# A two-layer attention-and-retention trunk: fixed rounds for the first supertiles' norms and tables, casts moved to ScalarE, a first rotation read from PSUM

## The chip, the cores and the metric

The kernel runs on one core of a Trainium2 chip. The time is that of one execution on the device, in microseconds (us). Five engines work side by side, each through a list of instructions of its own: TensorE (PE in the profile, its weight loads PEld), VectorE (DVE), ScalarE (ACT), GpSimd (POOL) and SyncE (SP), which issues the DMA transfers. An instruction waits on semaphores for what others must have done, and everything behind it on its engine waits too.

## The reference, cut to what matters

```python
# x (1, 2048, 1024) f32; two layers; rms_norm with a gain; chunks of 64 tokens
def hybrid_layer(x, norm_gain, w_in, w_out, rel_bias, cos, sin):
    hn = rms_norm(x, norm_gain)
    proj = hn @ w_in                                  # 1024 -> 8 sections of 512
    aq, ak, av, ag, rq, rk, rv, rg = jnp.split(proj, cuts, axis=-1)
    ya = chunked_rel_attention(aq, ak, av, rel_bias)  # 8 heads x 64, own chunk and 8 before
    yr = chunkwise_retention(rq, rk, rv, cos, sin)    # 4 heads x 128: rotary on q and k,
                                                      # decay inside a chunk, a running state,
                                                      # rms norm of each head's output
    y = jnp.concatenate([ya * silu(ag), yr * silu(rg)], axis=-1)
    return x + y @ w_out
def reference(x, positions, norm_gain, w_in, w_out, rel_bias, final_gain):
    cos, sin = rotary_tables(positions, RET_HEAD_DIM)
    for layer in range(2):
        x = hybrid_layer(x, norm_gain[layer], w_in[layer], w_out[layer], rel_bias[layer], cos, sin)
    return rms_norm(x, final_gain)
```

## The kernel before

Every large product is made of three float16 products: an operand is scaled by a power of two and split into a high and a low half, and high x high, high x low and low x high are added in PSUM. The scale of a weight section comes from the sum of its squares: ScalarE squares the section and adds up each row (`sumsq`), a cast to bfloat16 follows (`lowp`, on VectorE), one small matmul with ones adds over the 128 partitions (`allsum`), VectorE makes the scale (`norm_scale`), ScalarE writes the scaled high half and VectorE the low half (`convert`).

The 2048 tokens are four *supertiles* `n` of 512, each four tiles of 128 tokens; tile t, of 0 to 15, is called token t in the code's manner below. A layer is four passes `s` over all supertiles; a pass holds two attention heads and one retention head. Stage `(l, s, n)` is `dense_T`, which makes the four sections j = 0 to 3 whose output has features on the partitions (attention queries, attention keys, retention queries, retention keys; 24 matmuls each), and `dense_V`, which makes the values and gates, a section of 24 matmuls for each tile `a` of 128 tokens. Both use two PSUM buffers in turn (`psD`), so a section starts when the one before the last has been emptied: in `dense_V` by four ScalarE activations and three VectorE operations (`rests`, the lines of `v`, `rv` and `gt`). The matmuls of the attention and the retention of the stage before are put in between: `run` takes one step of the dense generator (8 matmuls, a *round*), then fires what `later` has put off to that round, one step of `attention`, and some steps of the background work in `bg`, as many as are needed to end it in time: preparing the next weights (`prep_T`, `prep_V`, `prep_O`), the output weights' maximum (`prep_Omax`), and in the first pass also the norms and the tables of cosines and sines of later supertiles (`norms_from_input`, `tables`).

A rotation (`evacuate`, j = 2 and 3) is made so: ScalarE copies the section out of PSUM into `raw`, two DMAs copy it with its halves exchanged into `swp`, the tables come by two more DMAs (`tab_load`), VectorE makes two products and a sum, and the result is split into halves. For keys a DMA transposes it into tokens (`tokens`).

The first stage is written out by hand, in the string that `do` reads: norms of tiles 0 to 3, the first weights, and the dense sections, as their inputs come. The first supertile's `dense_T` is computed in pieces of 128 tokens for j = 0 and 1. The tokens 4 to 7 follow as background work while the first `dense_V` runs (`push(rounds(...), 12)`), their rows go through a DMA transpose into the layout that `dense_T` reads (`hTh`, `hTl`). Tokens 8 to 15 follow in the stages behind (`push(norms_from_input(...), 21)`), each step with one step of the next table; their rows use the buffers `sc` and `pq` that the attention's scores use too. `decayed` makes the first product of the retention; for the first stage it is called from `attention`, for others from a fixed round.

PE, ACT, DVE and POOL run in the order in which the program is written; SP's order is that of the program in the first stage and a scheduler's afterwards. Names in the profile leave out numbers: `dT` is a section of `dense_T`, `dV` of `dense_V`, `hTh<-hTl` a transpose of rows that lie in a tile of the name `hTl`, `ms` the sum over partitions, `mb` its cast input, `swp` the exchanged halves.

Of the kernel before, what the change touches and what calls it, by code (L numbers as in the profile page):

```python
# [27 lines left out]
def hybrid_trunk(ctx: ExitStack, tc: tile.TileContext, x, pos, gain, gcol, w_in, w_out, rel, fgain,  # L28
# [107 lines left out]
    TAB_STEPS = 19  # L136

# [23 lines left out]
    def gain_scale(l):  # L161
# [7 lines left out]
        mb = lowp(ss, f"g{l}")  # L169
# [8 lines left out]
        mb = lowp(ss, f"h{l}")  # L178
# [126 lines left out]
    def sumsq(sts, nm, dst):  # L305

        m1 = b2.tile([P, len(sts)], F32, tag="m1", name=f"m1{nm}", bufs=4)
        for i, (st, k0, k1) in enumerate(sts):
            act.activation(st if dst is None else dst[:, k0:k1, :], st, AF.Square, accum_out=m1[:, i:i + 1])
        if len(sts) == 2:  # L310
            dve.tensor_tensor(m1[:, 0:1], m1[:, 0:1], m1[:, 1:2], op=ALU.add)
        return m1[:, 0:1]

    def lowp(m1, nm):
        mb = b2.tile([P, 1], BF16, tag="mb", name=f"mb{nm}", bufs=4)
        dve.tensor_copy(mb, m1)
        return mb

# [32 lines left out]
    class Sections:  # L351
# [16 lines left out]
        def square(self, j):  # L368
            nm = f"{self.nm}{j}"
            self.sq[j] = lowp(sumsq(self.sts[j], nm, self.g.h[:, j]), nm)  # L370
# [43 lines left out]
    def prep_V(l, s, g):  # L414
# [25 lines left out]
        for j in range(2):  # L440
            yield
            m1[j] = lowp(sq(j), f"{nm}{j}")
# [9 lines left out]
        m3 = sq(3)  # L452
        dve.tensor_tensor(m2, m2, m3, op=ALU.add)
        m2 = lowp(m2, f"{nm}2")
# [10 lines left out]
    def prep_V_next(l, g):  # L465
# [13 lines left out]
        m = [lowp(sumsq(sts[j], f"{nm}{j}", hi[j]), f"{nm}{j}") for j in range(2)]  # L479
        yield  # L480
        m2, m3 = (sumsq(sts[j], f"{nm}{j}", hi[j]) for j in (2, 3))
        dve.tensor_tensor(m2, m2, m3, op=ALU.add)
        m.append(lowp(m2, f"{nm}2"))
# [10 lines left out]
    def prep_Omax(l, go):  # L494
        nm = f"O{l}"
        mm = b2.tile([P, 1], F32, tag="omax", name=f"omax{nm}")
        st = load_sec(w_out[l, :, 0:P], f"{nm}m0")
        for j in range(KT):
            yield
            m1 = sumsq(st, f"{nm}m{j}", None)  # L500
            if j + 1 < KT:
                st = load_sec(w_out[l, :, (j + 1) * P:(j + 2) * P], f"{nm}m{j + 1}")
            if j == 0:
                dve.tensor_copy(mm, m1)
            else:
                dve.tensor_tensor(mm, mm, m1, op=ALU.add)
        mm = lowp(mm, nm)
        for _ in range(4):
            yield
# [98 lines left out]
    def dense_T(l, s, n, g, st):  # L608
# [17 lines left out]

        def evacuate(j, ps):
# [27 lines left out]
            else:  # L655
                w = 5 - j
                rot = b2.tile([P, w, 512], F16, tag=f"rot{j}", name=f"rot{nm}_{j}")
                if j == 2:
# [5 lines left out]
                def swap(rot=rot, raw=raw, j=j):  # L664
# [20 lines left out]
                    d = 5 if j == 2 and first else 3  # L685
# [7 lines left out]
                    else:  # L693
                        later(d + 5 if first else 11, tokens)

                if j == 2:
                    st.rq = rot
                    swap()
                    if first:
                        later(1, tab_load)  # L700
                else:
                    st.rk = rot
                    later(8 if first else 2, swap)
# [14 lines left out]
        for j in range(2 if first else 0, 4):  # L718
            if j == 2 and not first:
                tab_load()  # L720
# [57 lines left out]
    def attention(l, s, n, g, st, prev, nxt):  # L778
# [61 lines left out]
        for i, (a, hx) in enumerate(units):  # L840
# [11 lines left out]
            elif a == 0 and (l, s, n) == (0, 0, 0):  # L852
                decayed(l, s, n, g, st, 0)
# [297 lines left out]

    def run(gen, att, thirds):
        left = thirds
        for _ in gen:
# [3 lines left out]
            ring["att_done"] = att[0] is None  # L1158
            todo = sum(max(b[1], 0) for b in bg)
# [6 lines left out]
    def norms_from_input(ts, spaces, tab):  # L1166

        def load(k):
            u = us[k]
            u.x = spaces[k] if spaces else w4.tile([P, D], F32, tag="w4", name=f"xin{u.t}")  # L1170
            sp.dma_start(u.x, x[u.t * P:(u.t + 1) * P, :])

        def sq(k):
            u = us[k]
            u.h = [h_[:, :, u.t % 4 * P:(u.t % 4 + 1) * P] for h_ in hT_of(0, u.t // 4)]
            u.ss = squares(u.x.rearrange("p (k c) -> p k c", c=P), u.nm, u.h[0])

        def root(k):
            us[k].rs = rms_of(us[k].ss, gains[0].m, gains[0].e, us[k].nm)

        def mul(k):
            u = us[k]
# [333 lines left out]
```

## Time and profile before

| | us |
|---|---|
| median of 3 runs | 2095.43 (2093.11 to 2095.86) |
| the profiled execution | 2094.75 |
| its span, first to last instruction | 2092.8 |
| mean granted TensorE clock | 0.991 |
| TensorE busy in the span | 2004.4 |
| VectorE, ScalarE, GpSimd busy | 1343.8, 1141.3, 432.9 |

The profile is of one execution. Busy time is given for each engine; a row of a timeline has the start, the time that the merged instructions took, engine, source line, operation, what is written from what, the shapes, the count, and in brackets how long the engine stood idle before and what ended that. A group has busy time, the mean of one in ns, and the idle time before its instructions. The lines that carry the argument stand in the prediction.

### The profile page before, as it was taken

To read this page: it belongs to the slowest core of one execution; us is meant where nothing else is said; L and a number is where in the kernel's file an instruction comes from. 1 tells how busy PE (TensorE), PEld (TensorE's weight loads), DVE (VectorE), ACT (ScalarE), POOL (GpSimd) and SP (SyncE) were. 2 spreads that over 40 slices of the span, in tenths; PEclk is the share of its full clock that TensorE was granted. 3 is DMA by queue.
4 is the path that set the end of the run, shared out by engine and by line. 5 is a ranking of instruction groups with operands and counts; after the bars stand their busy time and mean duration, and the time that the engine had idled before them with its cause. 6 is when DMAs were issued, how large, how long until landed. Compare 5 with 4: busy or idle time off the path is not lost.

```text
span 2092.8 us, 39599 instructions
## 1 busy us (share of the span) xinstructions
PE 2004.4 (96%) x14014; PEld 1049.4 (50%) x14014; DVE 1343.8 (64%) x4031; ACT 1141.3 (55%) x2522; POOL 432.9 (21%) x509
## 2 busy tenths in 40 slices
PE   6888999999999999998999999999999999998998
PEld 4344455555555555444444555555555555554443
DVE  7676666666656666576654666666666667656643
ACT  7455665556565654455444546554655565455432
POOL 1022222222122212121000222222222222222100
PEclk9999999999999999999999999999999999999999
DMA  8767674557476764599965556655655776558874
GB/s 247 171 127 162 136 166 114 115 112 159 110 169 133 161 166 99 113 211 260 219 185 113 120 102 142 130 121 106 155 123 118 178 156 162 117 100 183 212 199 123
DMA packets 645702, 313.65 MB, mean 150 GB/s; under 512 B 459232, under 2 KB 602080, under 8 KB 645504
## 3 DMA queue, kind: packets, MB, share of 16 engines
q1 hardware_dynamic: 645504, 311.12, 66.4%
q8 instruction: 110, 1.80, 0.4%
q14 instruction: 88, 0.72, 0.1%
HBM read 123.26 MB, written 41.98 MB: 79 GB/s over the span
## 4 chain that ended last, share of the span: by engine, by line
PE 55%; DMA 7%; DVE 5%; ACT 3%; issue 1%; SPq 1%; POOL 0%; POOLq 0%; DVEq 0%; ACTq 0%
PE dT L731 18%; PE dV L752 15%; PE dO L1105 12%; DMA pT<-pq 2%; PE r L860 2%; PE S L801 2%; PE S L800 2%; PE o L820 1%; PE o L821 1%; PE o L822 1%; DVE sc L804 1%; DMA swp<-rot 1%; DMA yhy<-rhy 1%; ACT sc L807 1%; ACT pq L809 1%
## 5 line engine op out<-in xcount | busy, mean ns | idle before, releaser
L810 POOL TENSOR_TENSOR pq<-sc,pq 128x640 f16<-128x640 f32 (+4 forms) x256 | 323.8, 1265 | 1175.9 <-issue 590.7
L807 ACT ACTIVATE sc<-sc,mq,cT 128x640 f32<-128x640 f32 (+4 forms) x256 | 218.5, 853 | 558.1 <-DVE mq L806 413.7
L752 PE MATMUL dV<-whV,hTh 128*128 128x512 f16 x1024 | 354.5, 382 | 13.0 <-DVE gt L770 12.8
L731 PE MATMUL dT<-hTh,whT 128*128 128x512 f16 x1008 | 349.4, 382 | 14.7 <-DMA hTh<-hTl 9.6
L752 PE MATMUL dV<-wlV,hTh 128*128 128x512 f16 x1024 | 354.1, 381 | 0.0
L752 PE MATMUL dV<-whV,hTl 128*128 128x512 f16 x1024 | 354.0, 381 | 0.0
L731 PE MATMUL dT<-hTl,whT 128*128 128x512 f16 x1008 | 346.6, 379 | 0.0
L731 PE MATMUL dT<-hTh,wlT 128*128 128x512 f16 x1008 | 346.6, 379 | 0.0
L752 PEld LDWEIGHTS <-hTh 128*128 128x128 f16 x2048 | 197.3, 98 | 227.7 <-DVE gt L770 16.4
L731 PEld LDWEIGHTS <-whT 128*128 128x128 f16 x2016 | 192.9, 98 | 221.6 <-issue 24.1
L804 DVE CUSTOM_DVE_ANT_0 sc<-S,bias 128x640 f32<-128x640 f32 (+4 forms) x256 | 188.4, 736 | 78.8 <-PE S L801 61.1
L1105 PE MATMUL dO<-whO,yly 128*128 128x512 f16 x512 | 194.1, 379 | 2.4 <-DMA yly<-rly 2.4
L1105 PE MATMUL dO<-whO,yhy 128*128 128x512 f16 x512 | 194.0, 379 | 1.2 <-DVE gt L770 0.6
L1105 PE MATMUL dO<-wlO,yhy 128*128 128x512 f16 x512 | 194.0, 379 | 0.0
L809 ACT ACTIVATE pq<-sc 128x640 f16<-128x640 f32 (+4 forms) x256 | 171.5, 670 | 10.9 <-DMA pT<-pq 3.0
L1105 PEld LDWEIGHTS <-yhy 128*128 128x128 f16 x1024 | 99.6, 98 | 115.1 <-issue 0.8
L752 PEld LDWEIGHTS <-hTl 128*128 128x128 f16 x1024 | 99.7, 98 | 105.0 <-issue 2.8
L800 PE MATMUL S<-k,q 128*128 128x128 f16 (+3 forms) x592 | 143.1, 268 | 7.9 <-DVE mq L804 7.9
L731 PEld LDWEIGHTS <-wlT 128*128 128x128 f16 x1008 | 97.2, 98 | 101.8 <-issue 1.1
L820 PE MATMUL o<-v,pT 128*128 128x65 f16 x1120 | 129.6, 193 | 10.2 <-DMA pT<-pq 9.7
L801 PE MATMUL S<-k,q 128*128 128x128 f16 (+3 forms) x592 | 130.5, 268 | 0.0
L820 PEld LDWEIGHTS <-pT 128*128 128x128 f16 x1120 | 105.3, 97 | 49.2 <-DMA pT<-pq 21.3
(350 smaller groups left out, 3352.7 us busy)
## 6 DMA issues: line engine op xcount, KB each, us to landing
q<-qq SPq DMA_DIRECT2D x128, 128.0 KB, 2.7
yyy<-y_d SPq DMA_DIRECT2D x32, 512.0 KB, 4.6
stT<-in_w_in_dram SPq DMA_DIRECT2D x27, 512.0 KB, 4.8
stV<-in_w_in_dram SPq DMA_DIRECT2D x26, 512.0 KB, 4.5
k<-kk SPq DMA_DIRECT2D x128, 64.0 KB, 2.0
swp<-rot SPq DMA_DIRECT2D x64, 128.0 KB, 2.5
tabc<-tab SPq DMA_DIRECT2D x32, 256.0 KB, 2.7
tabs<-tab SPq DMA_DIRECT2D x32, 256.0 KB, 2.9
```

The lines of the kernel that those rows point to most:

```text
L731: pe.matmul(ps, w_[:, j, kt, :], h_[:, kt, :], start=(m == 0), stop=(m == 23))
L752: pe.matmul(ps, h_[:, kt, a * P:(a + 1) * P], w_[:, kt, :], start=(m == 0), stop=(m == 23))
L800: pe.matmul(o, st.q[:, hx, 0, cs], k_, start=True, stop=False)
L801: pe.matmul(o, st.q[:, hx, 1, cs], k_, start=False, stop=True)
L804: dve.tensor_tensor_reduce(out=v, in0=S[:, 0:w], in1=g.bias[hx][:, 640 - w:640], scale=1.0, scalar=-3.0e38, op0=ALU.add, op1=ALU.max, accu ...
L807: act.activation(v, v, AF.Exp, bias=m[:, 0:1], scale=g.c[:, 0:1])
L809: act.activation(pq[:, 0:w], v, AF.Copy)
L810: pool.tensor_tensor(pq[:, w:2 * w], v, pq[:, 0:w], op=ALU.subtract)
L820: pe.matmul(o[:, 0:65], u.p[:, b, :], v_[:, 0:65], start=(b == 0), stop=False)
L821: pe.matmul(o[:, 0:64], u.p[:, b, :], v_[:, 65:129], start=False, stop=False)
L860: pe.matmul(out_, w_, m_, start=(i == 0), stop=(i + 1 == len(pairs)))
L1105: pe.matmul(ps, h_[:, kt, :], w_[:, kt, :], start=(m == 0), stop=(m == 23))
```

## The change

Casts: `lowp` becomes a ScalarE activation; where a sum has two parts the second is added as its bias, and the VectorE addition is dropped (in `gain_scale` the cast stays on VectorE). `prep_Omax` keeps the eight sums of squares in eight columns, loads two sections ahead, adds them with one reduction, and is spread over the whole of the stage `n` = 2.

```diff
     def lowp(m1, nm, more=None):
         mb = b2.tile([P, 1], BF16, tag="mb", name=f"mb{nm}", bufs=4)
-        dve.tensor_copy(mb, m1)
+        if more is None:
+            act.activation(mb, m1, AF.Copy)
+        else:
+            act.activation(mb, m1, AF.Identity, bias=more[:, 0:1])
         return mb
...
     def prep_Omax(l, go):
+        ms = b2.tile([P, KT], F32, tag="omax", name=f"omax{nm}", bufs=1)
+        load(0)
+        load(1)
+        yield
         for j in range(KT):
-            yield
-            m1 = sumsq(st, f"{nm}m{j}", None)
-            if j + 1 < KT:
-                st = load_sec(w_out[l, :, (j + 1) * P:(j + 2) * P], f"{nm}m{j + 1}")
-            if j == 0:
-                dve.tensor_copy(mm, m1)
-            else:
-                dve.tensor_tensor(mm, mm, m1, op=ALU.add)
+            if j + 2 < KT:
+                load(j + 2)
+            yield
+            act.activation(st[j], st[j], AF.Square, accum_out=ms[:, j:j + 1])
+            yield
+        yield
+        dve.tensor_reduce(m1, ms, axis=AX.X, op=ALU.add)
```

First rotation: for the first stage the two products read the section in PSUM; the exchange of halves is made by the output's partitions, in two operations of 64 partitions each, and the copy out of PSUM and the four DMAs fall away. `decayed` of the first stage moves to round 10, that is into `dense_V`.

```diff
+        def first_rotation(j, ps, rot):
+            def cosine():
+                dve.scalar_tensor_tensor(out=own, in0=ps, scalar=2.0 ** -16, in1=st.tabc, op0=ALU.mult, op1=ALU.mult)
+            def sine(half):
+                i_, o_ = slice((1 - half) * 64, (2 - half) * 64), slice(half * 64, half * 64 + 64)
+                dve.scalar_tensor_tensor(out=st.swp[o_], in0=ps[i_], scalar=-2.0 ** -16, in1=st.tabs[i_], op0=ALU.mult,
+                                         op1=ALU.mult)
+            d = 2 * j
+            later(d, cosine)
+            later(d, lambda: sine(0))
+            later(d + 1, lambda: sine(1))
+            later(d + 2, lambda: dve.tensor_tensor(own, own, st.swp, op=ALU.add))
+            later(d + 3, lambda: act.activation(rot[:, 0], own, AF.Copy))
+            later(d + 4, lambda: dve.tensor_tensor(rot[:, 1], own, rot[:, 0], op=ALU.subtract))
```

Second supertile: j = 0 and 1 of stage (0, 0, 1) are made in pieces of 128 tokens, those of tokens 4 to 6 ahead of those of token 7, and both are emptied behind the last piece.

```diff
+        parts = (l, s, n) == (0, 0, 1)
+        if parts:
+            for (j, a) in ((0, 0), (0, 1), (0, 2), (1, 0), (1, 1), (1, 2), (0, 3), (1, 3)):
+                cs = slice(a * P, (a + 1) * P)
+                for i in range(24):
+                    w_, h_ = ((g.h, hh), (g.l, hh), (g.h, hl))[i // KT]
+                    pe.matmul(ps[j][:, cs], w_[:, j, i % KT, :], h_[:, i % KT, cs], start=(i == 0), stop=(i == 23))
+                    m += 1
+                    if m % 32 == 0 and m < 192:
+                        yield
+                if a == 3:
+                    evacuate(j, ps[j])
```

Fixed rounds: `run` counts rounds from the first `dense_V` on and fires what `slot` has put on a round. Up to round 95 the background work is pulled from there alone. A token's steps stand on set rounds (load 4 rounds ahead of its square, rows three to five rounds behind it), tokens 8 to 11 from round 18 and 12 to 15 from round 39, every three rounds; their rows lie in space of their own. The steps of the tables 1, 2 and 3 have set rounds, and the weights of pass 1 are prepared from round 57 on, 48 steps over 39 rounds.

```diff
+            for fn in slots.pop(ring["round"], ()):
+                fn()
+            ring["round"] += 1
+            if left is None:
+                continue
...
+            for i, fn in ((-4, load), (0, sq), (1, root), (2, mul), (3, lambda: rows_hi(rows, u.x)),
+                          (4, lambda: rows_lo(rows, u.x)), (5, lambda: transpose_rows(rows, *u.h))):
+                slot(r + i, fn)
+        for k, t in enumerate(ts):
+            v = rows[k % len(rows)].bitcast(F16)
+            token(t, r0 + 3 * k, (v[:, 0:D], v[:, D:2 * D]))
...
+    table_steps(t1, (12, 12, 13, 13, 14, 15, 17, 17))
+    table_steps(t2, [18] + list(range(22, 36)) + [36, 38, 38])
+    table_steps(t3, [36] + list(range(40, 54)) + [54, 56, 56])
+    norms_from_input(18, range(8, 12), late[0:4])
+    norms_from_input(39, range(12, 16), xs0[0:2])
+    first_prep = 57
+    for r in range(first_prep, 96):
+        for _ in range((r + 1 - first_prep) * 48 // 39 - (r - first_prep) * 48 // 39):
+            slot(r, lambda: pull(1))
+    slot(first_prep - 1, lambda: push(prep_T(0, 1, grp(0, 1)), 25))
...
-                if (l, s) == (0, 0) and 0 < n < NS - 1:
-                    if n == 1:
-                        push(t1, TAB_STEPS - 10)
-                    push(norms_from_input(range(4 * n + 4, 4 * n + 8), late[0:4] if n == 1 else None,
-                                          tables(n + 1, [xs0[n + 1][:, i * 256:(i + 1) * 256] for i in range(4)])), 21)
...
-                if (n, s) == (0, 0) and not first:
+                if (n, s) == (0, 0):
                     later(11, lambda n=n, g=g, st=st: decayed(l, s, n, g, st, 0))
```

154 lines of the change are left out of this document (82 added, 72 removed).

## The prediction

> **What bounds the kernel now.** I read the page's first part, then the busy time of each engine by stage, then who TensorE waited for in the early stages, then the timelines of the engines named there.
>
> ```profile
> PE 2004.4 (96%) x14014; PEld 1049.4 (50%) x14014; DVE 1343.8 (64%) x4031; ACT 1141.3 (55%) x2522; POOL 432.9 (21%) x509
> ```
>
> TensorE is the bound: of the span of 2092.8 us it is idle 88 us. The columns below are the stretch, its length, and the busy time (and count) of PE, PEld, DVE, ACT and POOL, the granted clock, the DMA share and GB/s. The cuts are mine: the wait after the first supertile, the second supertile, the third, the fourth with what follows, the rest.
>
> ```profile
> 69.10:78.90 9.80, 0.17 (x1) 0.02 (x1) 2.47 (x7) 1.21 (x4) 0.00 (x0) 0.62 1.08 241
> 78.90:140.10 61.20, 51.66 (x292) 24.67 (x292) 46.40 (x135) 35.14 (x75) 10.86 (x18) 0.95 0.62 130
> 140.10:204.90 64.80, 55.23 (x399) 29.32 (x399) 46.54 (x127) 36.24 (x76) 15.61 (x18) 0.94 0.74 154
> 204.90:360.00 155.10, 147.09 (x1081) 77.87 (x1082) 100.76 (x361) 94.09 (x217) 34.56 (x41) 0.99 0.65 141
> 360.00:2092.80 1732.80, 1698.38 (x11852) 885.03 (x11849) 1094.34 (x3264) 926.89 (x2061) 364.84 (x411) 1.00 0.66 147
> ```
>
> Between 69.1 and 360 us TensorE idles 9.6 + 9.5 + 9.6 + 8.0 = 36.7 us. In the 1732.8 us behind that it idles 34.4 us, and the change touches little there. The waits of TensorE from 60 to 142 us, from 142 to 206 and from 206 to 360 (total, times, longest):
>
> ```profile
> PE dT L731 <- DMA hTh<-hTl: 9.6, 1, 9.6
> PE dV L752 <- DVE gt L770: 5.5, 2, 4.9
> PE dT L731 <- issue: 2.2, 1, 2.2
> ...
> PE dV L752 <- DVE gt L770: 4.8, 2, 4.3
> PE dT L731 <- DMA hTh<-rhn: 2.8, 1, 2.8
> ...
> PE msT L323 <- DVE mbT L316: 3.3, 3, 1.9
> PE msV L323 <- DVE ya L832: 2.9, 2, 1.6
> ```
>
> Norm rows that land late, value sections whose accumulator VectorE empties late, and a sum that waits for a cast on VectorE: the places that the change edits. A wait also costs afterwards (start, duration, [idle before]):
>
> ```profile
> 78.91 3.26 PE L731 MATMUL dT<-hTh,whT 128*128 128x512 f16 x8 [9.64 <-DMA hTh<-hTl]
> ...
> 82.11 1.89 PE L731 MATMUL dT<-hTh,wlT 128*128 128x512 f16 x8
> ...
> 140.13 1.89 PE L731 MATMUL dT<-hTh,whT 128*128 128x512 f16 x8 [2.21 <-issue]
> ...
> 204.90 3.40 PE L731 MATMUL dT<-hTh,whT 128*128 128x512 f16 x8 [2.81 <-DMA hTh<-rhn]
> ```
>
> Eight matmuls take 1.89 us, but 3.26 and 3.40 behind waits of 9.64 and 2.81 us, and 1.89 behind one of 2.21: between 2.21 and 2.81 us the clock is halved for a while. By the clocks of the table that is 3.1 us of the second supertile (5% of 61.2; 1.4 of them at 78.91) and up to 3.9 of the third (6% of 64.8), of which I take 2.6, since a part of the slow stretch falls into the wait itself; and 1.5 at 204.9 (3.40 against 1.89). So 36.7 + 7.2 = 43.9 us are lost between 69 and 360 us.
>
> **The first rotation and the parts.** The change takes four copies by DMA and the loads of tokens 8 to 11 out of SP's queue ahead of the last rows of tokens 4 to 7.
>
> ```profile
> 70.71 0.57 SPq L1171 DMA_DIRECT2D hTh<-in_x_dram  x1
> ...
> 71.86 0.50 SPq L666 DMA_DIRECT2D swp<-raw  x1
> ...
> 73.10 1.53 SPq L236 DMA_TRANSPOSE hTh<-hTl  x1
> 74.73 2.92 SPq L237 DMA_TRANSPOSE hTl<-hTl  x1
> ```
>
> Those last two transposes end the 9.64 us wait; DMA engines are full (1.08) just there. Their rows were ready long before:
>
> ```profile
> 58.10 1.22 DVE L276 TENSOR_TENSOR hTh<-hTh,hTh 128x1024 f16<-128x1024 f32 x1
> 59.24 0.69 DVE L670 TENSOR_TENSOR rot<-rot,tabc 128x512 f32<-128x512 f32 x1
> ...
> 60.98 1.28 DVE L254 SCALAR_TENSOR_TENSOR hTl<-hTl,rsn,gb 128x1024 f32<-128x1024 f32 x1
> 62.17 0.68 DVE L670 TENSOR_TENSOR swp<-swp,tabs 128x512 f32<-128x512 f32 x1
> 62.77 0.28 DVE L766 SCALAR_TENSOR_TENSOR v<-dV,v 128x128 f16<-128x128 f32 x1
> ...
> 64.16 1.22 DVE L276 TENSOR_TENSOR hTl<-hTl,hTl 128x1024 f16<-128x1024 f32 x1
> ```
>
> By the new order of VectorE the queue turns around here. From start to start an L276 takes 1.14 us, an L254 1.19, a 512-wide product 0.60. Ahead of the second value section's evacuation (L766 at 62.77) stood two L276, one L254 and two products; now two L276, one L254 and six products or sums (first rotation: cosine, two halves of the sine, sum; second: cosine, one half). That is 58.10 + 2.28 + 1.19 + 3.65 = 65.2, and 0.8 for the evacuation: 66.0. The fourth section needs that accumulator:
>
> ```profile
> 63.93 0.38 PE L752 MATMUL dV<-whV,hTh 128*128 128x512 f16 x1
> ...
> 68.89 0.38 PE L752 MATMUL dV<-wlV,hTh 128*128 128x512 f16 x1
> ```
>
> So it starts at 66.0 instead of 63.9: a new wait of 2.1 us. The first decay product moves ahead too, behind two thirds of that section (69.5), and needs the second rotation. VectorE after 66.0: a sine half 0.6, L276 1.14, a lower part 0.6, a sum 0.6, two table steps 0.6, an evacuation 0.8, three table steps 0.95, the lower part 0.6: 71.9. A second wait, 2.4 us. The section ends at 66.0 + 5.2 + 2.4 = 73.6. The last rows are ready at 67.8, so two transposes of 1.3 us and some 3 us of flight put them at 71 to 73: no wait is left for the parts to save. TensorE goes on at 73.6 instead of 78.9: **-5.3**, and -1.4 of clock (3.26 against 1.89). Bounds: -11 if VectorE keeps up, 0 if it loses another 5 us.
>
> The products now read PSUM. The same 512-wide form from PSUM is in the groups:
>
> ```profile
> L634 DVE SCALAR_TENSOR_TENSOR qq<-dT,qq 128x512 f16<-128x512 f32 x32 | 21.9, 683 | 12.4 <-ACT qq L631 12.4
> ```
>
> 683 ns, like the 0.69 and 0.68 from SBUF above, so I charge nothing more. [...]
>
> The parts: 192 matmuls of 128 columns for 48 of 512.
>
> ```profile
> 30.73 0.61 PE L712 MATMUL dT<-hTl,whT 128*128 128x128 f16 x8
> 31.18 0.61 PE L712 MATMUL dT<-hTh,wlT 128*128 128x128 f16 x8
> ```
>
> Eight take 0.45 us start to start: 192 take 10.8 against 48 x 0.216 = 10.4. **+0.4**.
>
> **Norms and tables in rounds, rows apart.** The work is the same; its rows no longer take the two buffers of the attention's scores, and the Sin step of the third supertile's table leaves the value sections:
>
> ```profile
> L121 ACT ACT_TABLE_LOAD x3 | 3.8, 1283 | 0.0
> ```
>
> One such load and one back, 2.6 us, stood ahead of the evacuation behind the 4.9 us wait. What is left is VectorE's load. Second supertile: TensorE's own work is 51.7 - 3.1 = 48.6 us; VectorE's is 46.4 less the second rotation's 2.6, so 90% of it. I also see a new jam: sixteen SP issues of the table, the queries and the keys (0.5 to 0.6 us each, as the rows above) stand ahead of the table's reload, some 5 us that VectorE waits at the first cosine. That uses the slack up, so I keep half of what was lost there (9.5 + 1.7 of clock): 5.5. **-5.7**. Third: 55.2 - 2.6 = 52.6 against 46.5, without that jam, and its successor's rows are ready seven rounds ahead; lost 9.6 + 2.6 + 1.5, kept 5: **-8.7**. Fourth and next: lost 8.0, weight work spread over 39 rounds; kept 4: **-4.0**. Bounds: all of it gone, or all of it kept.
>
> **Casts by ScalarE.** Five casts in the start and 51 behind it leave VectorE.
>
> ```profile
> L316 DVE CAST mbT<-m1T 128x1 bf16<-128x1 f32 x28 | 4.4, 156 | 36.9 <-ACT whT L309 36.7
> ```
>
> VectorE stood 36.7 us idle behind the squares for these casts alone. On ScalarE the cast follows its square at once; the sum on TensorE comes three rounds later. Hidden by those rounds behind 360 us, where VectorE is 63% busy: 0. Bounds -2 to +3.
>
> **The output weights' maximum.** Its running sum held VectorE behind a square that waited for a load, and TensorE behind that:
>
> ```profile
> 623.55 0.19 DVE L506 TENSOR_TENSOR omaxO<-omaxO,m1O0m 128x1 f32<-128x1 f32 x1 [3.14 <-ACT stO0m L309]
> ```
> ```profile
> PE r L860 <- DVE dT L868: 2.4, 2, 1.3
> ...
> PE msO L323 <- DVE yr L925: 1.3, 2, 0.7
> ```
>
> These two waits, once a layer, are 3.7 us; with columns, one reduction and loads two ahead I keep 1.1: **-2.6**. Bounds -3.7 to +1.
>
> **The sum** against the profiled execution's 2094.75 us (1.95 around its span): -5.3 - 1.4 + 0.4 - 5.7 - 8.7 - 4.0 - 2.6 = -27.3, so 2067.5. The median shown is 0.7 above that execution: 2068.
>
> **Rivals.** (1) VectorE binds the second and third supertile, at 90% of TensorE's own work: what was lost there (11.2 + 13.7) stays, only the other terms gain, 12.9: 2083 with the 0.7. For it: every new wait I found ends on VectorE. Against: its idle time behind ScalarE goes. 0.22. (2) No wait is left between 63 and 360 us: 43.9 + 3.7 - 0.4 gained: 2048. For it: the DMA and buffer couplings named in the waits are cut. Against: the two waits worked out above. 0.09. (3) It does not do what it says: VectorE is so late that the rows and the decay product come when they did, and later waits move one supertile on: 2095. 0.07. (4) Slower: the sums wait for casts in ScalarE's queue, behind exponentials and Sin. Each of the three mbT waits cost 1.1 us (3.3 over 3); 51 casts at that price are 56 us, less the 27.3: 2124. It decides from 0.54 us a cast. Against: ScalarE is 53% busy behind 360 us and the sum comes three rounds after. 0.10. [...]
>
> **How the numbers follow.** The forecast has 0.52 and a range of its own from 2058 to 2078. 2054 to 2090 takes in rival 1, and leaves out most of 2, 3 and 4. A measurement tells 0.2%, 4 us, from no change. Faster: 0.52 + 0.22 + 0.09 = 0.83; same: 0.07; slower: 0.10.
>
> **What would show it.** Right: the fourth value section of the first supertile starts near 66 us, a wait of 2 to 3 us stands before the first decay product, the first part starts at 72 to 75 us without a wait for rows; the third supertile starts near 128 and the fourth near 183; no wait for the maximum above 1 us. Wrong: waits for `gt` of 4 us and more with half clock behind them, a wait of the parts for transposes, or sums that wait for ScalarE's cast in the later stages.

## The result and the profile after

The changed kernel is slower, by a third of a per cent, where the forecast was 27 us faster.

| | before | after |
|---|---|---|
| median, us | 2095.43 (19 runs, 2090.72 to 2100.03) | 2102.21 (19 runs, 2096.17 to 2105.39) |
| ratio after to before, 95% interval | | 1.0034 (1.0026 to 1.0043) |
| profiled execution, us | 2094.75 | 2103.35 |
| its span, us | 2092.8 | 2101.6 |
| mean granted clock | 0.991 | 0.993 |

The ratio is taken between runs of the two kernels on the same chip. The page's first part of after, and its row of the DMA queue of kind "instruction" (packets, MB, share), which comes up again below:

```profile
PE 2009.7 (96%) x14158; PEld 1058.0 (50%) x14158; DVE 1339.1 (64%) x3950; ACT 1151.0 (55%) x2576; POOL 433.2 (21%) x509
...
q8 instruction: 111, 1.82, 0.4%
```

The parts show as 144 more matmuls. VectorE has 81 instructions fewer and ScalarE 54 more, most of it the casts (e1 below, which has the casts alone, has 69 fewer and 56 more). Now the busy time by stage of after, cut where the prediction cut it, at the places where the supertiles begin here (columns as there):

```profile
60.00:75.70 15.70, 10.76 (x51) 4.54 (x50) 15.27 (x30) 5.96 (x14) 0.58 (x4) 1.00 0.80 165
75.70:135.76 60.06, 50.72 (x434) 30.36 (x433) 42.19 (x124) 31.09 (x71) 10.22 (x15) 0.97 0.56 124
135.76:200.11 64.35, 55.00 (x399) 28.53 (x399) 44.34 (x125) 38.26 (x78) 16.11 (x17) 0.97 0.82 175
...
357.00:2101.60 1744.60, 1701.84 (x11874) 886.09 (x11872) 1090.75 (x3209) 937.74 (x2109) 363.28 (x411) 1.00 0.66 147
```

TensorE still idles 60.06 - 50.72 = 9.3 us in the second supertile (9.5 before) and 9.4 in the third (9.6). Behind 357 us it idles 42.8, where before it idled 34.4 behind 360. The waits of TensorE in after, from 60 to 142 us, 142 to 206, 206 to 330, and in the stretch of the first layer's maximum, 575 to 640 (total, times, longest):

```profile
PE dV L819 <- DVE gt L837: 4.7, 2, 2.7
PE S L867 <- DVE mq L871: 3.4, 3, 2.7
PE dT L798 <- DVE ya L899: 3.0, 1, 3.0
PE r L925 <- DVE rot L668: 2.0, 1, 2.0
...
PE S L867 <- DVE mq L871: 2.7, 2, 2.1
PE dV L819 <- DVE gt L837: 2.3, 2, 2.1
PE dT L798 <- DVE gt L837: 2.2, 1, 2.2
...
PE msV L327 <- DVE yr L990: 2.6, 1, 2.6
PE dV L819 <- ACT whV L334: 2.2, 1, 2.2
...
PE o L887 <- DMA pT<-pq: 1.6, 2, 1.1
```

The 9.64 us for late rows is gone, and so is every wait of 4 us and more. In their place stand many of 2 to 3 us, and up to 206 us all that are shown end on VectorE. VectorE is at work while TensorE stands there: of the 17.8 us of TensorE's waits over half a microsecond that end between 75.7 and 200.2 us it is busy for 16.2. Before, of the 28.4 us that end between 78.9 and 205 us, it was busy for 11.3. In TensorE's timeline of after:

```profile
67.76 0.39 PE L819 MATMUL dV<-whV,hTh 128*128 128x512 f16 x1 [2.70 <-DVE gt L837]
...
73.91 0.23 PE L925 MATMUL r<-rot,rot 128*128 128x128 f16 x1 [2.03 <-DVE rot L668]
...
75.70 0.61 PE L775 MATMUL dT<-hTh,whT 128*128 128x128 f16 x8
...
135.76 1.89 PE L798 MATMUL dT<-hTh,whT 128*128 128x512 f16 x8 [2.97 <-DVE ya L899]
...
283.42 0.16 PE L327 MATMUL msV<-mbV,ones 128*128 128x1 bf16 x1 [2.63 <-DVE yr L990]
...
291.64 3.47 PE L819 MATMUL dV<-whV,hTh 128*128 128x512 f16 x8 [2.23 <-ACT whV L334]
```

The second supertile starts at 75.70 instead of 78.91, the third at 135.76 instead of 140.13, the fourth at 200.11 instead of 204.90. The dense products of stage (0,1,0), which follows the fourth supertile, end at 318.7 before and 319.0 after: the whole lead is given back in that one stage. From there to the end is 1774.1 before and 1782.6 after. By the prediction's terms, as differences of these places:

| stretch | predicted | measured |
|---|---|---|
| up to the second supertile's start (78.91, 75.70) | -5.3 | -3.2 |
| second supertile (61.20, 60.06 long) | -1.4 + 0.4 - 5.7 = -6.7 | -1.1 |
| third (64.80, 64.35) | -8.7 | -0.5 |
| fourth and (0,1,0), to 318.7 and 319.0 | -4.0 | +5.1 |
| from there to the end (1774.1, 1782.6) | -2.6 | +8.5 |
| sum | -27.3 | +8.8 |

The last row is the largest miss: a stretch that the change was said to touch little. Most of its +8.5 lies in the five stages that open a pass with loaded bias tables, (0,2,0), (0,3,0), (1,1,0), (1,2,0) and (1,3,0), each from the end of one stage's value sections to the end of its own: 265.7 us together before, 271.7 after.

### The profile page after: what moved, and what is told of

Same layout as the page of the kernel before. It is cut to its first block, busy times and chain, and to the rows that moved or that the text cites. A ratio compares the mean times of both kernels' runs of the same rounds, so it can differ in the third digit from the quotient of the medians.

```text
span 2101.6 us, 39837 instructions
## 1 busy us (share of the span) xinstructions
PE 2009.7 (96%) x14158; PEld 1058.0 (50%) x14158; DVE 1339.1 (64%) x3950; ACT 1151.0 (55%) x2576; POOL 433.2 (21%) x509
## 3 DMA queue, kind: packets, MB, share of 16 engines
q8 instruction: 111, 1.82, 0.4%
## 5 line engine op out<-in xcount | busy, mean ns | idle before, releaser
L798 PE MATMUL dT<-hTh,whT 128*128 128x512 f16 x992 | 342.9, 380 | 6.0 <-DVE ya L899 3.0
L867 PE MATMUL S<-k,q 128*128 128x128 f16 (+3 forms) x592 | 142.4, 267 | 11.8 <-DVE mq L871 11.8
L933 DVE SCALAR_TENSOR_TENSOR sh<-sh,state 128x128 f16<-128x128 f16 x120 | 96.1, 801 | 66.6 <-ACT sh L929 66.4
```

The source lines that it names most:

```text
L798: pe.matmul(ps, w_[:, j, kt, :], h_[:, kt, :], start=(m == 0), stop=(m == 23))
L867: pe.matmul(o, st.q[:, hx, 0, cs], k_, start=True, stop=False)
L933: dve.scalar_tensor_tensor(out=dst[:, 1], in0=dst[:, 0], scalar=-2.0 ** 11, in1=src, op0=ALU.mult, op1=ALU.add)
```

## Experiments

The ratios are taken against the kernel before on the same chip. The medians come from several chips, on which before alone took 2094.86 to 2097.6, so that they can't be compared with each other; "five stages" is that sum of lengths in the run's trace. Each run's profile is one execution, whose time behind 319 us scatters by some us, so that a verdict rests on the ratio and its interval, and the trace says where.

**Casts.** e1 is the kernel before with the first hunk of the change alone; e2 is after with that hunk undone.

```diff
-        dve.tensor_copy(mb, m1)
+        if more is None:
+            act.activation(mb, m1, AF.Copy)
+        else:
+            act.activation(mb, m1, AF.Identity, bias=more[:, 0:1])
```

> The kernel before with one edit alone: the casts by ScalarE (and the second part of a sum as the cast's bias). My prediction charged this edit 0 (bounds -2 to +3). Theory A (SP's queue): this edit alone moves one store in SP's order, y_d11<-ya, from behind the transpose pT of unit (3, 0, 1) and the first key copies to ahead of them, at the start of each later pass; the store waits for VectorE, and TensorE waits behind it, as at 699.32 and 1508.05 us in the changed kernel (2.86 and 2.48 us). Then this kernel takes 5 to 9 us more than the kernel before, 2100 to 2104, and its trace has waits of o for DMA pT at the starts of passes. Theory B (casts are free, the loss comes from other parts): 2095 within 2. Theory C (sums wait for the cast itself in ScalarE's queue): also slower, but the waits are of msT and msV for ACT mb.

> The changed kernel with the casts put back on VectorE; everything else of the change stays. Theory A: SP's order at the pass starts is the old one again, the 8 us lost behind 355 us come back: 2093 to 2096. Theory B: 2102. If VectorE's load in the second and third supertile matters, the casts there cost less than 1 us.

e1: 2097.9, 1.0006 (0.9997 to 1.0015). e2: 2103.14, 1.0034 (1.0022 to 1.0045), as after. The casts cost nothing that can be told from 0, by either way; the slow-down is elsewhere.

**SP's order.** In after SP issues a store of attention output ahead of a transpose of scores that TensorE waits for; e3 holds that store back.

```diff
+                i = sp.dma_start_transpose(out=u.p, in_=pq[:, 0:2 * w])
+                if (n, a, hx) == (3, 0, 1):
+                    tc.keep_in_program_order(i)
...
+                    if n == 2 and u.a == 3:
+                        later(4, store)
```

> The changed kernel with its casts on ScalarE, but the store of ya (supertile 2, tile 3) issued four rounds later and held behind the transpose of unit (3, 0, 1) in SP's order; nothing else moves. Theory A: the waits for pT at 521, 596, 699, 733, 1508 us go: 2093 to 2097. Theory C: the casts themselves cost the time, so it stays at 2101 to 2103.

2106.49, 1.0045 (1.0032 to 1.0058), five stages 273.1: no gain. SP's order there isn't the cause.

**Weights of pass 1 earlier.** 

```diff
-    first_prep = 57
+    first_prep = 51
```

> The changed kernel with the weights of pass 1 prepared from round 51 instead of 57, at the same rate, so done by round 90 instead of 95. Theory D: the lead of 7.3 us that the change has at 255 us is lost in stage (0, 1, 0) because the last conversions end only as their dense_V starts: the waits at 283.42 and 291.64 us (2.63 and 2.23) and the halved clock behind both (some 1.7 each) go, and the time falls by 5 to 8 us, to 2094 to 2097. Rival E: the weights' work meets the third supertile's norms six rounds sooner on VectorE and loses there what it gains: 2101 to 2103.

2110.21, 1.0063 (1.0051 to 1.0076). The waits of 2.63 and 2.23 us go and stage (0,1,0) takes 55.5 us for 60.7. But the third and fourth supertile grow by 10.5 together: from 190 to 330 us e4's waits of TensorE begin with

```profile
PE msT L327 <- ACT mbT L315: 11.5, 2, 8.7
```

a sum that stands 8.7 us for ScalarE's cast. That is rival 4's mechanism, in a place where the change as it stands does not have it (1.2 at most). So the weight work can be put against one stage or the other, and what it needs is not free in either.

**Semaphores.** SP's transfers use eight completion semaphores in turn (in the traces 1402 transfers before and 1398 in after, 174 to 176 on each); the change could have turned which transfer shares one with which. Four tiny loads, whose data nothing uses, are added in (0,1,1), to after (e5) and to before (e6).

```diff
+                if (l, s, n) == (0, 1, 1):
+                    for k in range(4):
+                        later(8 + k, lambda k=k: tiny(k))
```

> The changed kernel with four tiny loads (128 x 1) added in stage (0, 1, 1), behind the keys' copies; nothing else moves. Transfers take eight completion semaphores in turn, and the change issues four transfers fewer in the first stage (the two exchanges of halves of the first rotations), so that every later transfer has another of the eight than before. Theory F: that turn sets how long the same chain of transfers takes at the start of a pass (kt, toep, toep, bias, weights, pT), and thereby the waits of o for pT at 521, 596, 699, 733 and 1508 us. With four loads more the turn is the old one again: the loss of about 8 us behind 355 us goes, 2094 to 2097. Rival G: the turn has nothing to do with it: 2102 to 2104, at most 2 us slower for the four issues.

> The kernel before with the same four tiny loads at the same place. Theory F: it takes on the changed kernel's turn of semaphores and loses 5 to 8 us at the starts of the passes: 2100 to 2104. Rival G: 2095 to 2098.

e5: 2107.48, 1.005 (1.0036 to 1.0065), five stages 272.2. e6: 2100.62, 1.0019 (1.0009 to 1.0028), five stages 265.6. e6 is 0.2% slower than before, clear of noise and inside the 2100 to 2104 that the theory gave for it; where it loses these 4 us isn't known. But its five stages are as long as before, and the same loads do not shorten after's: for the five stages, which it was to explain, the theory falls.

**VectorE's waits in the second supertile.** e7 issues the table loads at once, where `tab_load` was put off by three rounds; e8 moves the subtraction that makes the low rows of tokens 8 to 15 to GpSimd.

```diff
-                if (l, s) == (0, 0):
-                    later(3, tab_load)
-                else:
-                    tab_load()
+                tab_load()
```
```diff
-                          (4, lambda: rows_lo(rows, u.x)), (5, lambda: transpose_rows(rows, *u.h))):
+                          (4, lambda: pool.tensor_tensor(rows[1], u.x, rows[0], op=ALU.subtract)), (5, lambda: transpose_rows(rows, *u.h))):
```

> The changed kernel with the reload of the tables in the first pass at once, not three rounds later. VectorE's wait of 5.50 us for tabc at 103.19 us goes. Theory H (VectorE's one wait makes it late for what TensorE needs): the waits of S for mq at 110.23 (2.72) and of the fourth value section at 125.42 (2.00) shrink, with the half clock behind the first (1.7): 3 to 5 us ahead at 140 us, and as much at the third supertile. Rival I: VectorE is late for the sum of its work, and the waits only move: within 1 us at 140 us. In the whole time 0 to 8 us less than 2102.

> The changed kernel with the lower halves of the norms' rows of tokens 8 to 15 subtracted by GpSimd instead of VectorE: eight operations of 1.2 to 1.6 us leave VectorE in the second and third supertile (6 us in each). Rival 1 of the prediction (VectorE's load binds there): the idle time of TensorE in these two stages (6.2 and 10.3 us in the changed kernel) falls by 2 to 5 us each, 2094 to 2098. Rival I' (it is the order and the latency of single steps, VectorE being idle a quarter of that time): less than 1 us each, 2100 to 2103.

e7: 2109.84, 1.0063 (1.0047 to 1.0078), slower even than after. e8: 2105.08, 1.0038 (1.0024 to 1.0053). VectorE's longest wait between 78 and 140 us, in after and then in e7:

```profile
DVE rot L720 <- DMA tabc<-tab: 5.5, 1, 5.5
```
```profile
DVE rot L720 <- DMA swp<-rot: 6.5, 1, 6.5
```

The wait for the table, which the prediction had foreseen as some 5 us, goes, and the one for the exchanged halves behind it comes in its place, longer. In e8, TensorE's waits from 60 to 142 us:

```profile
PE dV L819 <- DVE gt L837: 5.9, 3, 2.7
PE dT L798 <- DMA hTh<-hTl: 3.4, 1, 3.4
PE S L867 <- DVE mq L871: 2.5, 3, 1.8
```

With less work on VectorE the waits for it stay, and one for rows joins them. So it isn't VectorE's load alone; no single edit tried here shortened the stage.

**Place of buffers.** The change moves later buffers down by 32 bytes (`bufs=1` of `omax`). e9 takes that back in after, e10 makes it in before.

```diff
-        ms = b2.tile([P, KT], F32, tag="omax", name=f"omax{nm}", bufs=1)
+        ms = b2.tile([P, KT], F32, tag="omax", name=f"omax{nm}")
```
```diff
-        mm = b2.tile([P, 1], F32, tag="omax", name=f"omax{nm}")
+        mm = b2.tile([P, 1], F32, tag="omax", name=f"omax{nm}", bufs=1)
```

> The changed kernel with one word less: the eight sums of the output weights' maximum in two buffers, as the one sum had before (bufs=1 is dropped). All instructions and their order on every engine stay as in the changed kernel. What moves is where buffers lie: in the changed kernel everything allocated behind that small tile (weights, rows' transposes hT, bias, the loads' space w4) begins 32 bytes lower in each partition than in the kernel before, at 32 over a multiple of 64, and with this word at a multiple of 64 as before. Theory J (place of the buffers): transfers into these buffers take longer at an odd multiple of 32, and the chains of transfers at the starts of the passes with them; the waits of o for pT at 521 to 733, 1291 and 1508 us go, and the time falls by 5 to 10 us, to 2093 to 2097. Rival K (the place does not matter): 2101 to 2104.

> The kernel before with one word more: that small tile in one buffer (bufs=1). All instructions and their order stay; the buffers behind it lie 32 bytes lower, as in the changed kernel. Theory J: it loses 6 to 12 us, most of it at the starts of the passes, with waits of o for pT of 1 to 3 us: 2101 to 2108. Rival K: 2095 to 2097.

e9: 2106.19, 1.0044 (1.0031 to 1.0056). e10: 2096.61, 0.9999 (0.999 to 1.0008). Nothing.

**Instruction fetches.** The pages' rows of the queue of kind "instruction", before and in e12 (below), beside after's above:

```profile
q8 instruction: 110, 1.80, 0.4%
```
```profile
q8 instruction: 112, 1.84, 0.4%
```

These are 110, 111 and 112 packets of 16 KB. TensorE's matmuls and weight loads are 2 x 14014 = 28028 and 2 x 14158 = 28316, and in e12 2 x 14270 = 28540: 255 to a packet in all three. With the 163 and 168 instructions of TensorE's sequencer they are 28191 before and 28484 in after, 256.3 and 256.6 to a packet. The starts of the packets are 17.7 and 17.8 us apart in the median. From these counts, not from the packets' size as the expectation of e11 has it, I read a packet as a fetch of TensorE's next instructions, and estimate 256 to a fetch. The parts put in 288 = 256 + 32 instructions, so that by this estimate each later fetch comes 32 instructions sooner. Counted from the issue of the first bias load (`toep`) in each of the five stages, fetches stood at 13.1 to 13.6 us in the first layer and 4.6 to 5.2 in the second; in after they stand at 9.5 to 10.6 and 0.0 to 0.2, upon transfers that a chain waits for. The DMA view of after, in a short stretch around that issue in stage (1,2,0) (queue and what it moved; then issues with KB and us from issue to landing):

```profile
q8 instruction: 1, 0.02, 3.7%
...
toep<-rel_d SPq DMA_DIRECT2D x1, 383.5 KB, 6.4
kt<-rot SPq DMA_TRANSPOSE x1, 4.7
```

and the same place before, where no row of that queue stands:

```profile
q1 hardware_dynamic: 1352, 0.39, 85.7%
...
toep<-rel_d SPq DMA_DIRECT2D x2, 383.5 KB, 5.0
kt<-rot SPq DMA_TRANSPOSE x1, 3.2
```

A fetch takes 1.03 us in the median, and here `kt` lands 1.5 us later. The other traces agree: at the starts of (1,1,0), (1,2,0) and (1,3,0) `kt` lands 3.1 to 3.4 us from its issue in all ten traces of this document with the fetches in the old place, and 4.2 to 4.9 us in all nine with them moved. SP's queue behind it, before (start, duration):

```profile
1487.93 1.39 SPq L683 DMA_TRANSPOSE kt<-rot  x1
...
1494.26 0.34 SPq L577 DMA_DIRECT2D bias<-toep  x1
...
1495.53 2.74 SPq L812 DMA_TRANSPOSE pT<-pq  x1
```

and after:

```profile
1492.54 1.40 SPq L733 DMA_TRANSPOSE kt<-rot  x1
...
1500.40 0.33 SPq L588 DMA_DIRECT2D bias<-toep  x1
...
1501.33 3.28 SPq L879 DMA_TRANSPOSE pT<-pq  x1
```

`bias` was issued as the first `toep` landed (1494.25 before, 1500.39 in after), with the transpose of scores behind it on SP: from `kt` to `pT` are 7.60 us before and 8.79 after, and `o` waits for `pT`. To tell the fetches from the parts' own work, tiny matmuls of one column on ones, whose results nothing uses, are put at the very start: 144 of them in before (e11, the parts' number), 112 in after (e12: 224 instructions, which with 288 make 512, two whole packets by the estimate). e13 is after without the parts, hence with the count of before.

```diff
+    for i in range(4):
+        wp = psR.tile([P, 512], F32, tag="small", name=f"wp{i}")
+        for _ in range(36):
+            pe.matmul(wp[:, 0:1], ones.to_broadcast([P, P]), ones, start=True, stop=True)
```
```diff
+    for i in range(4):
+        wp = psR.tile([P, 512], F32, tag="small", name=f"wp{i}")
+        for _ in range(28):
+            pe.matmul(wp[:, 0:1], ones.to_broadcast([P, P]), ones, start=True, stop=True)
```
```diff
-        parts = (l, s, n) == (0, 0, 1)
+        parts = False
```

> The kernel before with 144 matmuls of one column (ones x ones) ahead of everything, in the first microseconds, where TensorE stands idle for 5.18 us; nothing else moves. They are as many instructions as the parts of the second supertile add (192 matmuls for 48, each with its weight load: 288). Theory L (instruction fetch): a DMA queue of kind instruction moves 16 KB about every 18 us, 1.03 us each, 110 of them; by their size these are TensorE's instructions, 256 at a time, and 288 more move each such fetch some 32 instructions ahead: from 13 to 10 us and from 5 to 0 us behind the toep copies at the starts of the passes, into the flight of kt and pT. Then this kernel gets the changed kernel's late transfers, with waits of o for pT: it loses 4 to 8 us behind 355 us, 2100 to 2105. Rival M (what makes the transfers late is another part of the change): 2095 to 2099, at most 2 us slower for the tiny matmuls.

> The changed kernel with 112 such tiny matmuls at the start: with the 288 instructions of the parts these make 512 more than before, twice 256, so that the fetches fall where they fell before. Theory L: the waits of o for pT at 521, 596, 699, 733, 1291, 1508 us go, the loss behind 355 us with them: 2094 to 2098. Rival M: 2101 to 2105.

> The changed kernel without the parts: j = 0 and 1 of the second supertile as whole sections again; all else stays, and TensorE has as many instructions as before. Theory L: the fetches fall where they fell before, 2093 to 2098 in all. For the parts themselves: the last rows land at 71 to 73 us and TensorE came at 75.70, so the second supertile still starts without a wait above 1 us, and is 0.4 us shorter. Rival M: 2101 to 2104. If the parts did hide rows, a wait for hTh or hTl of 2 us and more stands at the start of the second supertile.

| | fetches | median, us | ratio | five stages, us |
|---|---|---|---|---|
| before | old place | 2095.43 | | 265.7 |
| e11 | moved | 2099.01 | 1.0009 (0.9998 to 1.0021) | 271.1 |
| after | moved | 2102.21 | 1.0034 (1.0026 to 1.0043) | 271.7 |
| e12 | moved back | 2095.95 | 0.9993 (0.9984 to 1.0003) | 268.3 |
| e13 | moved back | 2098.43 | 1.0007 (0.9996 to 1.0017) | 267.9 |

The same place in e11 has the fetch and the long flight, in e12 neither:

```profile
q8 instruction: 1, 0.02, 2.8%
...
toep<-rel_d SPq DMA_DIRECT2D x2, 383.5 KB, 5.7
kt<-rot SPq DMA_TRANSPOSE x1, 4.3
```
```profile
toep<-rel_d SPq DMA_DIRECT2D x2, 383.5 KB, 5.3
kt<-rot SPq DMA_TRANSPOSE x1, 3.2
```

Over 360 to 1900 us TensorE's waits for `pT` are, before, after and in e12:

```profile
PE o L820 <- DMA pT<-pq: 8.4, 9, 2.2
```
```profile
PE o L887 <- DMA pT<-pq: 16.7, 13, 2.9
```
```profile
PE o L891 <- DMA pT<-pq: 13.8, 11, 2.5
```

e12 does more work than after and is faster, its interval wholly below after's; e13 gets there by leaving the parts out, and in e11 the same kind of useless matmuls works the other way, on the flights and the five stages of the kernel before. What the three have in common is the count alone, so the place of the fetches is a cause. The other runs bear it out. The eight versions of the changed kernel with moved fetches have ratios of 1.0034 to 1.0063, the six with the fetches back 0.9986 to 1.0007. The five stages take 263.8 to 268.3 us in the ten traces with the old place and 268.8 to 273.6 in the nine with the new. From the end of stage (0,1,0) to the end of the program the means are 1776.6 and 1784.9 us; of the ten, the four of the kernel before and its variants have 1776.5, the six of the changed kernel 1776.6.

Four things limit it. e11's time is not told from no change, and its interval allows 0.21% at most. Only two places, 32 instructions apart, were compared. The path from a fetch to TensorE isn't clean: at the three starts of the second layer's passes the waits of `o` for `pT` add up to 1.8 us before, 4.2 in after and 3.5 in e11, but 3.6 in e12 too, where `kt` lands in time, so that the transposes of scores were late there for another reason; over 360 to 1900 us the same waits come to 12.4 us in e11 and 15.7 in e13, nearly after's sum. And of the 5.3 us between the means of the five stages in the two groups of traces, 3.5 lie in (0,2,0) and (0,3,0), where `kt` is not slower and the fetch falls upon the first transpose of scores behind `toep` instead (in all nine, in none of the ten). Last, e13 ends 2.7 us above e12 in the profile, with the stages that hold the maximum, (0,2,2), (0,2,3), (1,2,2) and (1,2,3), 2.9 us longer; why stays open.

**With the fetches back.** e14 is e12 with the weight work of pass 1 in 36 rounds instead of 39. e15 is e14 with the old casts (as e2) and the old maximum. e16 is e14 with e3's edit, e17 is e16 with the old maximum.

```diff
-        for _ in range((r + 1 - first_prep) * 48 // 39 - (r - first_prep) * 48 // 39):
+        for _ in range((r + 1 - first_prep) * 48 // 36 - (r - first_prep) * 48 // 36):
```
```diff
-        ms = b2.tile([P, KT], F32, tag="omax", name=f"omax{nm}", bufs=1)
...
+        mm = b2.tile([P, 1], F32, tag="omax", name=f"omax{nm}")
...
+            if j == 0:
+                dve.tensor_copy(mm, m1)
+            else:
+                dve.tensor_tensor(mm, mm, m1, op=ALU.add)
```

> The changed kernel with 112 tiny matmuls, and with the weights of pass 1 prepared from round 57 at 48 steps in 36 rounds, not 39, so done by round 92. Theory L for the passes, and theory D for stage (0, 1, 0) in its milder form: the waits at 283.42 and 291.64 us and the half clock behind them go in part (3 us or more of 9.9), while the third and fourth supertile lose less than 2: 2090 to 2096. Rival E (what is taken away there is lost in the fourth supertile, as with the start at round 51): 2096 to 2103.

> 112 tiny matmuls and the faster weights of e14, and of the change only the first rotation, the parts and the fixed rounds: casts and the maximum as before the change. If casts and maximum are worth nothing (0 and at most 1 us each), it takes what e14 takes, 2094 to 2098. If the maximum in columns costs (its loads now stand in front of pT: 2.2 us idle in stage (0, 2, 2) against 1.2 before), it is 1 to 3 us faster than e14.

> e14 with the store of ya issued behind the transpose of unit (3, 0, 1), as in e3. Theory A in its smaller form: with the fetches out of the way the second pT of a pass comes 13 to 15 us behind the toep copies, against 12 in the kernel before, since the store waits ahead of it for VectorE; mended, the waits of o (0.4, 0.9, 0.8 us at 474, 683, 1488 us in e14) go, and 1 to 3 us with them: 2092 to 2095. Rival: the order is worth nothing, 2096.

> e16 with the output weights' maximum as before the change. If the maximum in columns gained what I predicted (2.6 us), this is 2 to 3 us slower than e16; if it costs at its new place, 1 to 2 us faster; with nothing either way, within 1 us.

| | median, us | ratio | five stages, us |
|---|---|---|---|
| e14 | 2096.39 | 0.9992 (0.9982 to 1.0001) | 264.8 |
| e15 | 2092.38 | 0.9986 (0.9976 to 0.9996) | 263.8 |
| e16 | 2093.98 | 0.9996 (0.9987 to 1.0005) | 267.5 |
| e17 | 2094.63 | 0.9997 (0.9989 to 1.0006) | 265.2 |

By their ratios all four lie below after, and within 0.15% of before. e16 lies no lower than e14, so that the store's order is worth nothing here either. e14's stage (0,1,0) is 4.7 us shorter than e12's (56.0 against 60.7) and its fourth supertile 4.9 longer (62.3 against 57.4): the weight work only moves again. e15 is the one version whose interval lies below 1: 0.14%, some 3 us, beats both kernels, but its difference from e14, e16 and e17 is within their intervals. The stages that hold the maximum take 213.2 us before and 214.5 in after, with the fetches back 216.4 (e14) and 213.8 (e16) with the new maximum, 214.3 (e15) and 214.0 (e17) with the old one: no gain of the new maximum shows.

## Why the prediction was wrong

The rotation, right in its mechanism. The fourth value section waited 2.70 us at 67.76 (predicted: 2.1 near 66), the first decay product 2.03 (2.4), the parts began at 75.70 (72 to 75) without a wait for rows, and VectorE stood 5.5 us for the table (some 5). The term came out at -3.2 for -5.3: the value section restarted 1.8 us later than the queue of VectorE had been worked out, and the rest followed from there. The products that read PSUM took 0.68 to 0.69 us, and the sum from SBUF beside them (at 64.81) 0.69: no price, as charged.

The parts: whether they cost 0.4 us isn't shown, since the intervals of e12 and e13 overlap. That no wait for rows was left for them to save was right: without them (e13) the second supertile starts at 75.45 us, and no wait stands ahead of it. What was missing is that 144 matmuls are also 288 instructions, and that the packets of the instruction queue (110 before, 111 in after) move with them.

The second and third supertile, wrong: -6.7 and -8.7 became -1.1 and -0.5. The step that failed is "I keep half of what was lost there". Idle time hardly moved (9.5 to 9.3 and 9.6 to 9.4); the waits of 4 to 10 us were split into waits of 2 to 3. That is rival 1 in its sum (11.2 lost there stays: 60.06 less the same 48.6 of TensorE's own work is 11.5), but only half in its reason. It said that VectorE binds by its load, and over the stage VectorE is busy for 42.19 of 60.06 us, 70%. Yet while TensorE stands VectorE is busy nearly throughout (16.2 of 17.8 us). It seems to work off what its own waits have held up, for tables, exchanged halves and scores: the 5.5 us for the table end at 103.2, and TensorE's 2.72 us for VectorE at 110.23. So I take it for a chain that goes to and fro between the engines; e7 and e8 each took one link out and found the next. Which chain sets the 60 us isn't settled. The half clock did not go either: TensorE worked 14.5 us at half clock between 69 and 360 us before, and 16.9 us between 75 and 357 in after.

The fourth and the next, wrong in sign: -4.0 became +5.1. The fourth supertile kept the lead (its end at 258.3 for 263.9), and (0,1,0) gave it back, with the waits of 2.63 and 2.23 us for the weights and half clock behind both. "Weight work spread over 39 rounds" was put down as a gain; it ends just where its user begins. e4 and e14 show that sooner isn't free either.

The casts, right: 0, by e1 and e2, and with them the judgement that rival 4 would not come. Only e4 shows what it looks like.

The maximum, wrong by its size: -2.6 became 0 or a little more. Its waits went, as predicted; waits of `o` for `pT` came in their place (1.6 us over two, in that stretch). What ended last there was not the wait that was removed alone.

The rest behind 360 us, the step that failed and turned the sign: "it idles 34.4 us, and the change touches little there". The order of the work there hardly changed, and that was all that was looked at. With the fetches back in place (e12, at most 0.03% above before) the change is worth about nothing; so the two halves of the miss are these: the gains of the first 320 us are given back to other waits, and the fetches' place goes with the 0.4% from e12 to after, 8.3 us behind stage (0,1,0) by the means of the two groups of traces. That it costs as much in any kernel isn't shown: in the kernel before (e11) it is 0.21% at most.

## What to carry to other kernels

A wait that is removed is worth only what the next-latest input leaves: before keeping half of it, follow the consumer's other inputs in the trace, above all where the engine named in the waits is itself not busy. Here 288 more instructions on TensorE, early in the program, put the packets of the instruction queue 3 to 5 us sooner at the starts of all five stages looked at; where an edit adds instructions, see where those packets fall, and compare variants at the same count. Where background work can only be moved from one stage to its neighbour, sum both stages before calling it a gain.

## What the runs showed of the hardware

The queue of kind "instruction" (q8) brought 16 KB about every 18 us (110 packets before, 111 in after), 1.03 us each: one packet for 255 of TensorE's matmuls and weight loads, which is why I take them for its instructions. That is 0.4% of the DMA time, yet the flight of `kt` at the start of (1,2,0) went from 3.2 to 4.3 us (e11) and 4.7 us (after) when one fell upon it. In the traces of before and after no `kt` with such a packet in its flight (13 of 64) landed in less than 3.9 us, and the median of the others is 3.2, though five of them took 4.4 to 5.3 too. In time, the ratio is 1.0034 in after against 0.9993 in e12.

Half clock did not follow from a gap's length alone: behind 2.23 us (at 291.64) eight matmuls took 3.47 us, behind 2.97 us (at 135.76) the same eight took 1.89. So the prediction's line "between 2.21 and 2.81" was no line.

What half clock went with in the traces of before and after is how the gap lies. The granted clock changed there only at points that are whole multiples of 3.41 us apart (13 changes before, 15 in after). Stretches of after cut at such points (busy time of PE first, the granted clock third from the end):

```profile
107.14:110.55 3.41, 0.69 (x9) 0.44 (x8) 3.34 (x10) 0.31 (x2) 0.33 (x2) 1.00 0.85 184
110.55:113.97 3.42, 3.42 (x10) 1.22 (x9) 2.47 (x8) 3.39 (x6) 0.91 (x1) 0.50 0.43 128
131.03:134.45 3.42, 1.59 (x14) 0.82 (x12) 3.42 (x10) 1.00 (x4) 0.55 (x1) 1.00 0.68 128
134.45:137.86 3.41, 2.10 (x21) 1.19 (x22) 2.34 (x13) 2.91 (x8) 1.15 (x1) 1.00 0.94 146
137.86:141.27 3.41, 3.41 (x24) 1.64 (x20) 2.83 (x12) 1.10 (x2) 0.00 (x0) 1.00 1.18 213
...
288.05:291.46 3.41, 1.36 (x13) 0.84 (x12) 3.20 (x12) 3.12 (x6) 0.00 (x0) 1.00 0.59 115
291.46:294.87 3.41, 3.23 (x8) 1.13 (x8) 2.67 (x5) 0.41 (x2) 0.00 (x0) 0.50 0.56 158
```

TensorE is idle for 2.72 us of the first stretch and 2.05 us of the one from 288.05, and has half clock in the next. The gap of 2.97 us is split: with an earlier one of 0.17 us, 1.83 us lie idle in one stretch and 1.31 in the next, and nothing follows. In these two traces, past the first 31 us, half clock followed every such stretch at full clock with 2.05 us idle or more (15 of them), and none with 1.94 or less; between the two none lay. The prediction's wait of 2.21 us at 140.13 was split too: at most 1.82 us of it lay in one stretch.
